# Attention keys stored in halves, and engine passes that take walked operands one half at a time

## The chip, the cores and the metric

The kernel runs on one core of one Trainium2 chip. The metric is the device time of one execution in microseconds (us). The core has TensorE (PE, with weight loads shown apart as PEld), VectorE (DVE), ScalarE (ACT), GpSimd (POOL) and SyncE (SP), which issues the transfers. PE writes into eight banks of PSUM; everything else lies in SBUF, 128 partitions deep.

## The reference

Two decoder layers over 256 tokens of width 1024, in float32. Layer 0 mixes tokens with a recurrent block, layer 1 with sparse attention; each is followed by a squared-ReLU MLP of width 4096, each sub-layer begins with an RMSNorm and ends with a residual add.

```python
# layer 0
proj = h @ w_in
y = gelu(proj[..., :D_RNN])
xb = conv4(proj[..., D_RNN:])                  # causal, depthwise
r = sigmoid(blockdiag(xb, w_a) + b_a); i = sigmoid(blockdiag(xb, w_x) + b_x)
a = exp(-8 * r * softplus(-lam)); u = sqrt(1 - a*a) * (i * xb)
x = x + (scan(a, u) * y) @ w_out
# layer 1: 16 heads in 4 groups, three branches, each with its own keys and values
s = q @ k.T * scale - slope * distance         # compressed, selected, window keys
o = g0 * softmax(s_c) @ v_c + g1 * softmax(s_s) @ v_s + g2 * softmax(s_w) @ v_w
x = x + o @ w_out
# after each
x = x + (relu(h @ w_up) ** 2) @ w_down
```

With 256 tokens all four blocks of 64 keys are selected and the window of 512 holds everything, so the selected and the window branch each see all causal keys. The compressed branch has 15 keys (16 with one of padding).

## The kernel before

**Products in split precision.** Activations lie transposed: model columns on partitions, tokens along the free axis. Each float32 operand is split into a high part (type float32r) and the rest. `mm3` (L328 to L330) multiplies high by high, high by low and low by high into one bank; `mm2` (L333, L335) does the same in two matmuls, where high and low parts lie side by side. Weights come by DMA into `raw`, a copy makes `whi`, a subtraction makes `wlo` (L278 and L287 in the MLPs, L341 and L338 in the planned sections; `copy` and `diff` are helpers, so many different passes carry L341 and L338).

**Walked operands.** A tile of 256 tokens is read by PE as 0, 128, 1, 129, and so on: one value of the first half, one of the second. `walk` and `walks` are that view, and `pairs` is the plain view with the same shape.

```python
def pairs(x):
    return x.rearrange("p (a i) -> p a i", i=2)
def walk(x):
    return x.rearrange("p (i a) -> p a i", i=2)
```

The bank then holds the tokens in the order 0, 128, 1, 129, ... Whoever reads it has to put them back: L679 (convolution input `xp`), L740 (gelu branch `y`), L796 (MLP up, `t`), L911 (queries), L923 (keys), L960 (keys and values before compression) read `pairs(z())`, multiply with `walk(rs)` (one over the norm, per token) and write `walk(...)`: they alternate between the halves at every value. In the other direction, tiles whose product shall come out in the plain order are stored so that the walk restores it: `xbh` and `xbl` (L341, L338 in `product`), `uhl` (L802, L803 after the up product), `oh` and `ol` (L341, L338 in `pv`).

**Sections.** The recurrent layer and the attention layer are each one `Section`: every operation is added to a planner with its engines, an assumed length in us, what it reads and writes, and a wished time. `emit` draws random offsets from a seed, makes a list schedule, improves it by backward and forward passes, takes the plan with the earliest end, and issues each engine's operations in that plan's order. Within an engine the order is then fixed, and engines wait for each other through semaphores. The MLPs are issued in program order: 32 pieces of the up product, each followed by `up_post` (L796, L801, L802, and L803 one piece later), then 8 x 4 pieces of the down product.

**End of the recurrent layer.** The `y` products come last. For each pair of chunks: L740 twice on DVE, gelu on ACT (L746), a product with the scan's result on DVE (L747), `xbh` (ACT or DVE) and `xbl` (DVE). The output projection needs all four pairs.

**Attention.** Per head three score products run (L1129 with the high part of the keys, L1130 with the low part): queries 0 to 127 against the first 128 keys of both branches and the compressed keys; queries 128 to 255 against the selected and the compressed keys; and against the window keys. Keys lie in `kh` and `kl`, group after group, in blocks of 128 keys in a row with the 16 compressed keys between them (`kset`, `kpair`, `kcomp`), and PE reads them in a row. DVE subtracts distances and finds the maximum from the bank (L1140; L1147 for compressed keys), ACT takes the exponential (L1143), DVE and ACT rescale (L1168, L1167), PE transposes (L1183), and `pv` (L1202) multiplies with values, two chunks of the output in one bank. `oh` and `ol` are made from that bank; the output projection of the last chunks waits for them.

Of the kernel before, what the change touches and what calls it, by code (L numbers as in the profile page):

```python
# [19 lines left out]
P = 128  # L20
# [199 lines left out]
def trunk_kernel(ctx: ExitStack, tc: tile.TileContext, x_in, vec_in, const_in, w2_in, wts, out):  # L220
# [320 lines left out]
    with ExitStack() as ph:  # L541
# [196 lines left out]
        def branch(m, t):  # L738
            z, zk = sec.proj("in", m, nextbank(), t, PJ)
            add("dve", 0.34, lambda e: e.tensor_tensor(walk(y_t[m]), pairs(z()), walk(rs), op=OP.mult), r=[zk, "rs"], w=[("y", m)], t=t + 2.6)  # L740

        def product(m, t):
            yk, hk, lk = keys("y", m), keys("xbh", m), keys("xbl", m)
            y, h, l_, x = (pair(z, m) for z in (y_b, xbhw, xblw, t_b))
            yw = y.rearrange("p k (a i) -> p k a i", i=2)
            add("act", 0.53, lambda e: e.activation(y, y, AF.Gelu_apprx_tanh), r=["tab"], w=yk, t=t)  # L746
# [37 lines left out]
    def mlp(layer, epilogue, first, last=None):  # L784
        with ExitStack() as ph:
# [4 lines left out]
            uhl = [up.tile([P, 2 * S], F32R, name="uhl", tag="uhl", bufs=NF) for _ in range(NF)]  # L790
            uh, ul = [walk(x[:, :S]) for x in uhl], [walk(x[:, S:]) for x in uhl]
            zrot = rotation(3, 4, 5, 0, 1, 2)

            def up_post(m, z):
                t = tmp.tile([P, S], F32, name="t", tag="t")
                dve.scalar_tensor_tensor(walk(t), pairs(z), 0.0, walk(rs), op0=OP.max, op1=OP.mult)  # L796
                flush()
# [3 lines left out]
                act.activation(u, t, AF.Square)  # L801
                act.activation(uh[m], pairs(t), AF.Square)  # L802
                later(lambda: dve.tensor_tensor(ul[m], pairs(u), uh[m].bitcast(F32), op=OP.subtract))  # L803

# [44 lines left out]
    with ExitStack() as ph:  # L849
# [15 lines left out]
        at.tile([P, 16], F32, name="edge0")  # L865
        GK, PC = 2 * S + NCP, P + NCP
        kh, kl = (at.tile([P, 4 * GK + NCP], F32R, name=n) for n in ("kh", "kl"))
        kpair = lambda y, g, n: y[:, g * GK:g * GK + 2 * (S + NCP)].rearrange("p (b k) -> p b k", b=2)[:, :, :n]
        kcomp = lambda y: y[:, :4 * GK].rearrange("p (g k) -> p g k", g=4)[:, :, P:PC]

        def kset(y, g, br):
            o, n = g * GK + br * (S + NCP), P if br else PC
            return y[:, o:o + 2 * n].rearrange("p (b k) -> p b k", b=2)[:, :, :P]
        two_blocks = lambda y: y.rearrange("p (b k) -> p b k", b=2)
# [30 lines left out]
        def qchunk(c, b, t, step):  # L905
# [4 lines left out]
            ak, bk = ("sa", c % NQ), ("sb", c % NQ)  # L910
            add("dve", 0.4, lambda e: e.scalar_tensor_tensor(walk(x), pairs(z()), cst[:, C_QS + c:C_QS + c + 1], walk(rs),  # L911
                                                             op0=OP.mult, op1=OP.mult), r=[zk, "rs"], w=[xk], t=t)
# [6 lines left out]
        def kchunk(gp, br, b, t, step):  # L919
            z, zk = proj_t(("ks", "kw")[br], gp, b, t, step)  # L920
            t += 4 * step
            x, xk, l_, lk = turn()
            add("dve", 0.34, lambda e, x=x: e.tensor_tensor(walk(x), pairs(z()), walk(rs), op=OP.mult), r=[zk, "rs"], w=[xk], t=t)  # L923
            x, l_ = two_blocks(x), two_blocks(l_)
# [31 lines left out]
        def cproj(i, gp, b, t, step):  # L956
            z, zk = proj_t(("ck", "cv")[i], gp, b, t, step)
            t += 4 * step
            x, xk, _, _ = turn()
            add("dve", 0.34, lambda e, x=x: e.tensor_tensor(walk(x), pairs(z()), walk(rs), op=OP.mult), r=[zk, "rs"], w=[xk], t=t)  # L960
            for hf in range(2):
# [144 lines left out]
        def scores(s, t):  # L1106
# [7 lines left out]
            a, cj = s // 4, s % 4  # L1114
            cview = lambda y, n, k: y[:, :2 * n].rearrange("p (b k) -> p b k", b=2)[:, :, :k]
            parts = ((0, lambda x: cview(x, PC, PC), lambda y: kpair(y, g, PC), (0, 1), 0.26),
                     (1, lambda x: x[:, :S + NCP], lambda y: y[:, g * GK:g * GK + S + NCP], (0,), 0.25),
                     (1, lambda x: x[:, :S], lambda y: y[:, g * GK + S + NCP:(g + 1) * GK], (1,), 0.23))
            for i, (qc, view, keys_, sets, d) in enumerate(parts):
# [12 lines left out]
                for b in sets:  # L1132
# [3 lines left out]
                    dist = cst[:, C_D0 + qc * P:C_D0 + qc * P + nk]  # L1136
                    src = (lambda z, b=b: cview(z(), PC, P)[:, b]) if qc == 0 else (
                        (lambda z: z()[:, :S]) if b else lambda z: cview(z(), PC, P))
                    shape = two_blocks if (qc, b) == (1, 0) else lambda y: y
                    add("dve", (0.2, 0.34)[qc], lambda e, z=z, src=src, shape=shape, dist=dist, row=row, j=j: e.tensor_tensor_reduce(  # L1140
                        shape(row), src(z), shape(dist), -slope, -NEG, OP.add, OP.min, mx[:, j:j + 1]),
                        r=bk + ["cst"], w=[mk, pk], t=t + 0.3)
# [3 lines left out]
                if 0 in sets:  # L1146
                    add("dve", 0.22, lambda e, z=z, qc=qc: e.tensor_tensor_reduce(  # L1147
                        css[a % 2][:, cj, qc], z()[:, P:PC], cst[:, C_DC + qc * NCP:C_DC + (qc + 1) * NCP], -slope, -NEG, OP.add,
                        OP.min, cmx[a % 2][:, 2 * cj + qc:2 * cj + qc + 1]),
# [288 lines left out]
```

## Time and profile before

| what | value |
|---|---|
| median of 3 runs | 562.9 us (562.57 to 563.83) |
| the profiled execution's own time | 563.95 us |
| its span, first to last instruction | 561.8 us |
| PE busy | 550.5 us (98%) |
| DVE busy | 436.3 us (78%) |
| ACT busy | 358.0 us (64%) |
| moved by DMA | 103.61 MB, mean 184 GB/s |
| granted PE clock over the span | 0.996 |

A matmul's length in the profile (about 276 ns for 256 columns) is longer than the distance to the next one, since matmuls overlap; the rate is read from the starts of successive ones. Passes of DVE and ACT overlap a little too, so that the next begins before the last has ended. Groups name a line, an engine, an operation, the tile written and the tiles read, the shape, the count, and then the busy time and the mean length of one in ns.

### The profile page before, as it was taken

The numbers are of one execution on the slowest core, as the hardware profiler recorded it, in microseconds if no ns is written. First come the engines' busy times: TensorE is split into PE (matmuls) and PEld (weight loads), VectorE is DVE, ScalarE is ACT, GpSimd is POOL, SyncE is SP. The second block draws the span as 40 slices with busy tenths as digits, with TensorE's granted clock in tenths as the row PEclk, the third lists the DMA queues.
The fourth block names the chain that finished last, engine by engine and source line by source line (L and its number), as shares of the span: only waits on it lengthen the run. The fifth ranks groups of instructions, "written<-read, shape, count | busy, mean of one in ns | idle before, by whom it ended". The sixth has DMA issues, their size and how long they took to land.

```text
span 561.8 us, 11456 instructions
## 1 busy us (share of the span) xinstructions
PE 550.5 (98%) x4422; PEld 528.5 (94%) x4422; DVE 436.3 (78%) x888; ACT 358.0 (64%) x670; POOL 40.1 (7%) x55
## 2 busy tenths in 40 slices
PE   9999899999999999999999999999999999999995
PEld 9989899999999999999899998989999999999995
DVE  6899999887788476476849999989988887465532
ACT  7699587777666354354646999977776765353321
POOL 1010000000000131131000000000000000142220
PEclk9999999999999999999999999999999999999998
DMA  8927266576566646655675432263586667556402
GB/s 313 409 90 226 83 225 215 174 234 200 191 194 222 223 161 214 225 167 198 219 229 177 143 104 58 76 211 99 200 239 200 191 213 234 182 187 218 158 1 76
DMA packets 33222, 103.61 MB, mean 184 GB/s; under 512 B 3856, under 2 KB 8080, under 8 KB 33168
## 3 DMA queue, kind: packets, MB, share of 16 engines
q1 hardware_dynamic: 32624, 102.42, 55.5%
q8 instruction: 35, 0.57, 0.4%
q10 hardware_dynamic: 544, 0.46, 0.2%
q14 instruction: 19, 0.16, 0.1%
HBM read 99.23 MB, written 1.05 MB: 179 GB/s over the span
## 4 chain that ended last, share of the span: by engine, by line
PE 73%; DVE 18%; DMA 5%; ACT 2%; issue 1%; SPq 0%; POOL 0%; DVEq 0%; ACTq 0%; POOLq 0%
PE bank L333 19%; PE bank L329 13%; PE bank L330 13%; PE bank L328 13%; PE bank L335 9%; DVE wlo L338 4%; DMA raw<-in_dram 3%; DVE pt L1140 2%; DMA gw<-in_dram 2%; DVE pt L1168 2%; DVE xb L683 1%; DMA pt<-tt 1%; DVE tt L911 1%; DVE t L735 1%; PE bank L1036 1%
## 5 line engine op out<-in xcount | busy, mean ns | idle before, releaser
L328 PE MATMUL bank<-hhl,whi 128*128 128x256 f32 x768 | 212.0, 276 | 0.4 <-DVE tt L960 0.4
L330 PE MATMUL bank<-hhl,wlo 128*128 128x256 f32 x768 | 211.5, 275 | 0.0
L329 PE MATMUL bank<-hhl,whi 128*128 128x256 f32 x768 | 211.5, 275 | 0.0
L333 PE MATMUL bank<-uhl,whi 128*128 128x512 f32 x480 | 157.3, 382 | 0.0
L328 PEld LDWEIGHTS bank<-hhl,whi 128*128 128x128 f32 x768 | 147.7, 192 | 0.6 <-DVE tt L960 0.4
L330 PEld LDWEIGHTS bank<-hhl,wlo 128*128 128x128 f32 x768 | 147.7, 192 | 0.0
L329 PEld LDWEIGHTS bank<-hhl,whi 128*128 128x128 f32 x768 | 147.7, 192 | 0.0
L287 DVE TENSOR_TENSOR wlo<-raw,whi 128x1024 fp32r<-128x1024 f32 x115 | 142.8, 1262 | 1.9 <-ACT whi L278 1.9
L335 PE MATMUL bank<-uhl,wlo 128*128 128x256 f32 x480 | 130.8, 273 | 0.0
L278 ACT CAST whi<-raw 128x1024 fp32r<-128x1024 f32 x116 | 120.0, 1056 | 14.1 <-ACT whi L278 11.0
L333 PEld LDWEIGHTS bank<-uhl,whi 128*128 128x128 f32 x480 | 90.7, 189 | 12.6
L335 PEld LDWEIGHTS bank<-uhl,wlo 128*128 128x128 f32 x480 | 92.2, 192 | 0.0
L338 DVE TENSOR_TENSOR wlo<-raw,whi 128x1024 fp32r<-128x1024 f32 (+2 forms) x72 | 77.1, 1091 | 1.9 <-ACT whi L341 1.8
L341 ACT CAST whi<-raw 128x1024 fp32r<-128x1024 f32 (+2 forms) x64 | 61.1, 969 | 15.4 <-DMA raw<-in_dram 7.3
L538 DVE TENSOR_TENSOR xt<-xt,bank 128x256 f32<-128x256 f32 x54 | 22.3, 419 | 62.2 <-PE bank L335 60.2
L796 DVE SCALAR_TENSOR_TENSOR t<-bank,rstd 128x256 f32<-128x256 f32 x64 | 39.5, 622 | 22.7 <-PE bank L330 22.6
L801 ACT ACTIVATE u<-t 128x256 f32<-128x256 f32 x64 | 26.7, 417 | 45.1 <-DVE t L796 44.9
L803 DVE TENSOR_TENSOR uhl<-u,uhl 128x256 fp32r<-128x256 f32 x64 | 40.8, 638 | 2.7 <-ACT uhl L802 2.6
L802 ACT ACTIVATE uhl<-t 128x256 fp32r<-128x256 f32 x64 | 42.5, 664 | 0.0
L514 ACT ACTIVATE hhl<-xt,vec 128x256 fp32r<-128x256 f32 x8 | 4.1, 508 | 41.4 <-DVE xt L538 41.4
L1143 ACT ACTIVATE pt<-pt,mx 128x128 f32<-128x128 f32 (+1 forms) x64 | 28.6, 449 | 2.0 <-DVE mx L1140 2.0
L1295 ACT ACTIVATE xg<-xt,vec 128x256 f32<-128x256 f32 x7 | 3.6, 508 | 37.7 <-DVE xt L538 37.7
(206 smaller groups left out, 764.1 us busy)
## 6 DMA issues: line engine op xcount, KB each, us to landing
raw<-in_dram SPq DMA_DIRECT2D x171, 512.0 KB, 4.3
raw<-in_dram SPq DMA_DIRECT2D x4, 560.0 KB, 4.5
gw<-in_dram SPq DMA_DIRECT2D x4, 512.0 KB, 9.2
raw<-in_dram SPq DMA_DIRECT2D x6, 256.0 KB, 4.9
y<-in_dram SPq DMA_DIRECT2D x2, 512.0 KB, 7.5
pT<-in_dram SPq DMA_DIRECT2D x2, 512.0 KB, 6.9
xt<-in_dram SPq DMA_DIRECT2D x3, 256.0 KB, 4.9
kl<-tl SPq DMA_DIRECT2D x8, 64.0 KB, 3.8
```

Of the source, the lines that this page charges most:

```text
L278: (act.copy if eng is None else eng.tensor_copy)(hi_t[i % NSPL][:, :n], raw_of(i)[:, :n])
L287: (eng or dve).tensor_tensor(lo[:, :n], raw_of(i)[:, :n], hi[:, :n].bitcast(F32), op=OP.subtract)
L328: pe.matmul(ps, wh, xh, start=start, stop=False)
L329: pe.matmul(ps, wh, xl, start=False, stop=False)
L330: pe.matmul(ps, wl, xh, start=False, stop=stop)
L333: pe.matmul(ps.rearrange("p (h a i) -> p h a i", h=2, i=2), wh, xhl.rearrange("p (h i a) -> p h a i", h=2, i=2), start=start, stop=False)
L335: pe.matmul(pairs(ps[:, S:]), wl, xh, start=False, stop=stop)
L338: return lambda e: e.tensor_tensor(o, a, h.bitcast(F32), op=OP.subtract)
L341: return lambda e: (e.copy if e is act else e.tensor_copy)(o, a)
L796: dve.scalar_tensor_tensor(walk(t), pairs(z), 0.0, walk(rs), op0=OP.max, op1=OP.mult)
L802: act.activation(uh[m], pairs(t), AF.Square)
L803: later(lambda: dve.tensor_tensor(ul[m], pairs(u), uh[m].bitcast(F32), op=OP.subtract))
```

## The change

It has two parts. First, every DVE or ACT pass with a walked operand keeps its data where they were and changes the order in which it goes through them. `evens` reads or writes all even places and then all odd ones; `parts` takes the first half and then the second. A pass that alternated between the halves of its SBUF tile and read a bank in a row now goes through the tile in a row and through the bank (or the other tile) at every second value. Second, the keys are stored in halves of a region of 272 places per group and branch: all even keys, and 136 places further all odd keys, the compressed keys in front of the selected ones in the same manner. The score products read the two halves alternately, which gives the plain order in the bank; the DVE passes on scores then read one run, where the first of queries 128 to 255 read two blocks. In the planner the assumed lengths of two of the three score products fall by 0.01.

```diff
+    def evens(x):
+        return x.rearrange("p (a i) -> p i a", i=2)
+    def parts(x):
+        return x.rearrange("p (i a) -> p i a", i=2)
...
-            add("dve", 0.34, lambda e: e.tensor_tensor(walk(x[:, 3:]), pairs(z()), walk(rs), op=OP.mult), r=[zk, "rs"], w=[xk], t=t)
+            add("dve", 0.34, lambda e: e.tensor_tensor(parts(x[:, 3:]), evens(z()), parts(rs), op=OP.mult), r=[zk, "rs"], w=[xk], t=t)
...
-            add("dve", 0.34, lambda e: e.tensor_tensor(walk(y_t[m]), pairs(z()), walk(rs), op=OP.mult), r=[zk, "rs"], w=[("y", m)], t=t + 2.6)
+            add("dve", 0.34, lambda e: e.tensor_tensor(parts(y_t[m]), evens(z()), parts(rs), op=OP.mult), r=[zk, "rs"], w=[("y", m)], t=t + 2.6)
...
-            y, h, l_, x = (pair(z, m) for z in (y_b, xbhw, xblw, t_b))
-            yw = y.rearrange("p k (a i) -> p k a i", i=2)
+            y, h, l_, x = (pair(z, m) for z in (y_b, xbh_b, xbl_b, t_b))
+            yw = y.rearrange("p k (a i) -> p k i a", i=2)
+            h, l_ = (z.rearrange("p k (i a) -> p k i a", i=2) for z in (h, l_))
...
-                dve.scalar_tensor_tensor(walk(t), pairs(z), 0.0, walk(rs), op0=OP.max, op1=OP.mult)
+                dve.scalar_tensor_tensor(parts(t), evens(z), 0.0, parts(rs), op0=OP.max, op1=OP.mult)
...
-                act.activation(uh[m], pairs(t), AF.Square)
-                later(lambda: dve.tensor_tensor(ul[m], pairs(u), uh[m].bitcast(F32), op=OP.subtract))
+                act.activation(uhp[m], evens(t), AF.Square)
+                later(lambda: dve.tensor_tensor(ulp[m], evens(u), uhp[m].bitcast(F32), op=OP.subtract))
...
+        KR, HC = S + NCP, NCP // 2
+        kh, kl = (at.tile([P, 8 * KR], F32R, name=n) for n in ("kh", "kl"))
+        kpair = lambda y, g: y[:, 2 * g * KR:2 * (g + 1) * KR].rearrange("p (r i q) -> p r q i", r=2, i=2)[:, :, :PC // 2]
+        kcomp = lambda y: y.rearrange("p (g r i q) -> p g r q i", g=4, r=2, i=2)[:, :, 0, :HC]
+        def kregion(y, g, br):
+            o = (2 * g + br) * KR
+            return y[:, o:o + KR].rearrange("p (i q) -> p i q", i=2)
+        def kplain(y, g, br):
+            o = 0 if br else HC
+            return kregion(y, g, br)[:, :, o:o + P]
+        def kall(y, g, br):
+            return kregion(y, g, br)[:, :, :P if br else P + HC].rearrange("p i q -> p q i")
...
-                add(HI, copy(kset(kh, g, br), x), r=[xk], w=[("k", g, br), ("k", g, br, 1)], t=t + 0.5)
+                add(HI, copy(kplain(kh, g, br), evens(x)), r=[xk], w=[("k", g, br), ("k", g, br, 1)], t=t + 0.5)
...
-            parts = ((0, lambda x: cview(x, PC, PC), lambda y: kpair(y, g, PC), (0, 1), 0.26),
-                     (1, lambda x: x[:, :S + NCP], lambda y: y[:, g * GK:g * GK + S + NCP], (0,), 0.25),
-                     (1, lambda x: x[:, :S], lambda y: y[:, g * GK + S + NCP:(g + 1) * GK], (1,), 0.23))
+            parts = ((0, lambda x: x[:, :2 * PC].rearrange("p (r q i) -> p r q i", r=2, i=2), lambda y: kpair(y, g), (0, 1), 0.25),
+                     (1, lambda x: pairs(x[:, :KR]), lambda y: kall(y, g, 0), (0,), 0.24),
+                     (1, lambda x: pairs(x[:, :S]), lambda y: kall(y, g, 1), (1,), 0.23))
...
-            ow = lambda: o().rearrange("p (k a i) -> p k a i", k=n, i=2)
+            ow = lambda: o().rearrange("p (k a i) -> p k i a", k=n, i=2)
...
-            add([("act", 0.1 + 0.24 * n, 0.0), ("dve", 0.07 + 0.27 * n, 0.2)], lambda e: copy(ohw[:, oj], ow())(e), r=bk, w=ok,
+            add([("act", 0.1 + 0.24 * n, 0.0), ("dve", 0.07 + 0.27 * n, 0.2)], lambda e: copy(ohp[:, oj], ow())(e), r=bk, w=ok,
...
-            add("dve", 0.07 + 0.27 * n, lambda e: diff(olw[:, oj], ow(), ohw[:, oj])(e), r=bk + ok, w=lk, t=t + 1.9 * n + 0.3)
+            add("dve", 0.07 + 0.27 * n, lambda e: diff(olp[:, oj], ow(), ohp[:, oj])(e), r=bk + ok, w=lk, t=t + 1.9 * n + 0.3)
```

The passes L911, L923 and L960 change in the same way as the one of `y`.

More of the change, by code (lines that the diff above doesn't have):

```diff
@@ L791, in mlp @@
             uh, ul = [walk(x[:, :S]) for x in uhl], [walk(x[:, S:]) for x in uhl]
+            uhp, ulp = [parts(x[:, :S]) for x in uhl], [parts(x[:, S:]) for x in uhl]
             zrot = rotation(3, 4, 5, 0, 1, 2)
@@ L865, in trunk_kernel @@
         at.tile([P, 16], F32, name="edge0")
[L866 to L874, printed above, removed]
+        PC = P + NCP
+        KR, HC = S + NCP, NCP // 2
[10 more added lines that the diff above has]
+            return kregion(y, g, br)[:, :, :P if br else P + HC].rearrange("p i q -> p q i")
         at.tile([P, 16], F32, name="edge1")
@@ L878, in trunk_kernel @@
         ohw, olw = (walks(x.rearrange("p (k s) -> p k s", s=S)) for x in (oht, olt))
+        ohp, olp = (x.rearrange("p (k i a) -> p k i a", i=2, a=P) for x in (oht, olt))
         oh, ol = ([x[:, i] for i in range(8)] for x in (ohw, olw))
@@ L910, in qchunk @@
             ak, bk = ("sa", c % NQ), ("sb", c % NQ)
-            add("dve", 0.4, lambda e: e.scalar_tensor_tensor(walk(x), pairs(z()), cst[:, C_QS + c:C_QS + c + 1], walk(rs),
+            add("dve", 0.4, lambda e: e.scalar_tensor_tensor(parts(x), evens(z()), cst[:, C_QS + c:C_QS + c + 1], parts(rs),
                                                              op0=OP.mult, op1=OP.mult), r=[zk, "rs"], w=[xk], t=t)
@@ L922, in kchunk @@
             x, xk, l_, lk = turn()
-            add("dve", 0.34, lambda e, x=x: e.tensor_tensor(walk(x), pairs(z()), walk(rs), op=OP.mult), r=[zk, "rs"], w=[xk], t=t)
-            x, l_ = two_blocks(x), two_blocks(l_)
+            add("dve", 0.34, lambda e, x=x: e.tensor_tensor(parts(x), evens(z()), parts(rs), op=OP.mult), r=[zk, "rs"], w=[xk], t=t)
             for hf in range(2):
                 g = gp * 2 + hf
-                add(HI, copy(kset(kh, g, br), x), r=[xk], w=[("k", g, br), ("k", g, br, 1)], t=t + 0.5)
-            add("dve", 0.34, diff(l_, x, kset(kh, gp * 2, br)), r=[xk, ("k", gp * 2, br), ("k", gp * 2, br, 1)], w=[lk], t=t + 1)
+                add(HI, copy(kplain(kh, g, br), evens(x)), r=[xk], w=[("k", g, br), ("k", g, br, 1)], t=t + 0.5)
+            add("dve", 0.34, diff(parts(l_), evens(x), kplain(kh, gp * 2, br)), r=[xk, ("k", gp * 2, br), ("k", gp * 2, br, 1)], w=[lk], t=t + 1)
             for hf in range(2):
                 own, oth, g = own_(hf), own_(1 - hf), gp * 2 + hf
-                move(kset(kh, g, br)[oth], kset(kh, g, br)[own], [("k", g, br)], [("k", g, br, 1)], t + 0.8)
-                move(kset(kl, g, br)[own], l_[own], [lk, "kl"], [("k", g, br, 2)], t + 1.2)
+                move(kplain(kh, g, br)[oth], kplain(kh, g, br)[own], [("k", g, br)], [("k", g, br, 1)], t + 0.8)
+                move(kplain(kl, g, br)[own], l_.rearrange("p (i q) -> p i q", i=2)[own], [lk, "kl"], [("k", g, br, 2)], t + 1.2)
         def kkeys(g, br):
@@ L959, in cproj @@
             x, xk, _, _ = turn()
-            add("dve", 0.34, lambda e, x=x: e.tensor_tensor(walk(x), pairs(z()), walk(rs), op=OP.mult), r=[zk, "rs"], w=[xk], t=t)
+            add("dve", 0.34, lambda e, x=x: e.tensor_tensor(parts(x), evens(z()), parts(rs), op=OP.mult), r=[zk, "rs"], w=[xk], t=t)
             for hf in range(2):
@@ L997, in kc_out @@
                 r=["hid"] + ck, w=[("ps", 6)], t=t)
-            o4 = lambda: o().rearrange("p (g n) -> p g n", g=4)
+            o4 = lambda: o().rearrange("p (g q i) -> p g q i", g=4, i=2)
             add("act", 0.1, lambda e: e.copy(kcomp(kh), o4()), r=[("ps", 6)], w=["kch"], t=t)
@@ L1114, in scores @@
             a, cj = s // 4, s % 4
-            cview = lambda y, n, k: y[:, :2 * n].rearrange("p (b k) -> p b k", b=2)[:, :, :k]
-            parts = ((0, lambda x: cview(x, PC, PC), lambda y: kpair(y, g, PC), (0, 1), 0.26),
-                     (1, lambda x: x[:, :S + NCP], lambda y: y[:, g * GK:g * GK + S + NCP], (0,), 0.25),
-                     (1, lambda x: x[:, :S], lambda y: y[:, g * GK + S + NCP:(g + 1) * GK], (1,), 0.23))
+            parts = ((0, lambda x: x[:, :2 * PC].rearrange("p (r q i) -> p r q i", r=2, i=2), lambda y: kpair(y, g), (0, 1), 0.25),
+                     (1, lambda x: pairs(x[:, :KR]), lambda y: kall(y, g, 0), (0,), 0.24),
+                     (1, lambda x: pairs(x[:, :S]), lambda y: kall(y, g, 1), (1,), 0.23))
             for i, (qc, view, keys_, sets, d) in enumerate(parts):
@@ L1136, in scores @@
                     dist = cst[:, C_D0 + qc * P:C_D0 + qc * P + nk]
[L1137 to L1141, printed above, removed]
+                    so = (0 if qc else PC) if b else NCP
+                    add("dve", (0.2, 0.34)[qc], lambda e, z=z, so=so, nk=nk, dist=dist, row=row, j=j: e.tensor_tensor_reduce(
+                        row, z()[:, so:so + nk], dist, -slope, -NEG, OP.add, OP.min, mx[:, j:j + 1]),
                         r=bk + ["cst"], w=[mk, pk], t=t + 0.3)
@@ L1147, in scores @@
                     add("dve", 0.22, lambda e, z=z, qc=qc: e.tensor_tensor_reduce(
-                        css[a % 2][:, cj, qc], z()[:, P:PC], cst[:, C_DC + qc * NCP:C_DC + (qc + 1) * NCP], -slope, -NEG, OP.add,
+                        css[a % 2][:, cj, qc], z()[:, :NCP], cst[:, C_DC + qc * NCP:C_DC + (qc + 1) * NCP], -slope, -NEG, OP.add,
                         OP.min, cmx[a % 2][:, 2 * cj + qc:2 * cj + qc + 1]),
```

## The prediction, made before the result was known

> **What bounds the kernel now.** I read the page's busy line first, then the waits of TensorE (PE), then the busy time by stretches.
>
> ```profile
> span 561.8 us, 11456 instructions
> ...
> PE 550.5 (98%) x4422; PEld 528.5 (94%) x4422; DVE 436.3 (78%) x888; ACT 358.0 (64%) x670; POOL 40.1 (7%) x55
> ```
>
> PE works through the whole span; only time that PE does not need or does not lose can leave the total. What it loses to other engines is listed by the view of waits (engine and line, what it waited for, total, times, longest):
>
> ```profile
> PE bank L329 <- DVE xbl L338: 1.2, 2, 1.0
> PE bank L329 <- DVE ol L338: 0.7, 1, 0.7
> PE bank L328 <- ACT xbh L341: 0.5, 1, 0.5
> PE bank L1036 <- DVE tt L960: 0.4, 1, 0.4
> PE bank L328 <- DVE tt L960: 0.4, 1, 0.4
> ...
> PE bank L1129 <- DVE cm L1147: 0.3, 1, 0.3
> ```
>
> All six waits are for operations that this change rewrites, or for a VectorE (DVE) queue that holds such operations. The stretches (us; busy time of PE, PEld, DVE, ACT, POOL with counts) say where that can matter:
>
> ```profile
> 65.60:72.50 6.90, 5.18 (x41) 4.46 (x39) 6.90 (x10) 3.99 (x5) 0.00 (x0) 1.00 0.71 230
> ...
> 95.00:180.00 85.00, 85.00 (x751) 84.64 (x750) 71.96 (x101) 60.36 (x99) 0.00 (x0) 1.00 0.62 203
> ...
> 372.50:377.00 4.50, 3.68 (x32) 3.05 (x29) 3.41 (x4) 3.50 (x4) 0.00 (x0) 1.00 0.96 353
> ```
>
> In the first (end of the recurrent layer) DVE is busy throughout and PE is not; in the second (up half of the first MLP) PE is busy throughout; in the third (end of attention) PE idles while ACT and DVE take turns.
>
> **The change part by part: the engines' order.** The groups by shape give the price of a walked pass (mean ns of one after the busy time):
>
> ```profile
> L803 DVE TENSOR_TENSOR uhl<-u,uhl 128x256 fp32r<-128x256 f32 x64 | 40.8, 638 | 2.7 <-ACT uhl L802 2.6
> L796 DVE SCALAR_TENSOR_TENSOR t<-bank,rstd 128x256 f32<-128x256 f32 x64 | 39.5, 622 | 22.7 <-PE bank L330 22.6
> L538 DVE TENSOR_TENSOR xt<-xt,bank 128x256 f32<-128x256 f32 x54 | 22.3, 419 | 62.2 <-PE bank L335 60.2 <-PE bank L330 1.4
> L740 DVE TENSOR_TENSOR y<-bank,rstd 128x256 f32<-128x256 f32 x8 | 4.9, 618 | 0.0
> L338 DVE TENSOR_TENSOR xbl<-y,xbh 128x512 fp32r<-128x512 f32 x4 | 4.4, 1099 | 0.1
> L338 DVE TENSOR_TENSOR ol<-bank,oh 128x512 fp32r<-128x512 f32 x4 | 4.4, 1093 | 1.1 <-ACT oh L341 1.1
> ```
>
> ```profile
> L802 ACT ACTIVATE uhl<-t 128x256 fp32r<-128x256 f32 x64 | 42.5, 664 | 0.0
> L801 ACT ACTIVATE u<-t 128x256 f32<-128x256 f32 x64 | 26.7, 417 | 45.1 <-DVE t L796 44.9
> L341 ACT CAST oh<-bank 128x512 fp32r<-128x512 f32 x4 | 4.4, 1093 | 0.2 <-PE bank L1202 0.2
> L341 ACT CAST xbh<-y 128x512 fp32r<-128x512 f32 x3 | 3.4, 1132 | 3.6 <-DVE y L747 3.6
> L746 ACT ACTIVATE y<-y 128x512 f32<-128x512 f32 x4 | 2.5, 632 | 3.1 <-DVE y L740 3.0
> ```
>
> L538 reads a bank too and has as many values as L740, but no operand is walked: 419 against 618 ns. On ACT, L801 and L802 square the same tile; the walked output costs 664 against 417. So jumping between the two halves at every value costs about 0.20 us per 256 values on DVE and 0.25 on ACT. After the change the same values go to the same places, one half at a time: outputs are written and rstd is read in a row, and the other operand (bank, t, u, y) is read at every second value. No row of this trace reads at every second value, so I bound it: from below by the unwalked rows (419 DVE, 417 ACT, a gain of 0.20 to 0.25), from above by a second penalty of the walk's size (about 0.82 on DVE, a loss of 0.20). I take the unwalked price: a step of two values is far nearer to neighbours than to a jump of 128, and the walked row is what happens at 128.
>
> [...]
>
> Where does it land? In the up halves, 64 groups save 0.4 us of DVE and 0.25 of ACT each, some 26 and 16 us of busy time, and I count **nothing**: PE is busy for 85.00 of 85.00 us there and no wait of PE in the list names L796, L802 or L803. What is covered stays covered, by PE's own 2.7 us per piece.
>
> **End of the recurrent layer.** These rows of the timeline (start, length) are PE's stall and the queue that makes it:
>
> ```profile
> 65.56 0.28 PE L330 MATMUL bank<-xbh,wlo 128*128 128x256 f32 x1
> 66.31 0.38 PE L328 MATMUL bank<-xbh,whi 128*128 128x256 f32 x1 [0.48 <-ACT xbh L341]
> 67.72 0.38 PE L329 MATMUL bank<-xbl,whi 128*128 128x256 f32 x1 [1.03 <-DVE xbl L338]
> ```
>
> ```profile
> 52.70 0.69 DVE L722 SCALAR_TENSOR_TENSOR t<-a,t 128x512 f32<-128x512 f32 x1
> ...
> 61.90 0.62 DVE L740 TENSOR_TENSOR y<-bank,rstd 128x256 f32<-128x256 f32 x1
> 62.35 1.11 DVE L338 TENSOR_TENSOR xbl<-y,xbh 128x512 fp32r<-128x512 f32 x1
> 63.30 1.22 DVE L338 TENSOR_TENSOR wlo<-raw,whi 128x1024 fp32r<-128x1024 f32 x1
> 64.43 0.68 DVE L747 TENSOR_TENSOR y<-y,t 128x512 f32<-128x512 f32 x1
> 65.03 0.61 DVE L740 TENSOR_TENSOR y<-bank,rstd 128x256 f32<-128x256 f32 x1
> ...
> 66.61 1.06 DVE L338 TENSOR_TENSOR xbl<-y,xbh 128x512 fp32r<-128x512 f32 x1
> ```
>
> ```profile
> 52.05 0.61 ACT L721 ACTIVATE a<-r 128x512 f32<-128x512 f32 x1
> ...
> 65.14 1.11 ACT L341 CAST xbh<-y 128x512 fp32r<-128x512 f32 x1 [1.95 <-DVE y L747]
> ```
>
> Start to start a walked 256 takes 0.45 (61.90 to 62.35) and a walked 512 takes 0.95; an unwalked 512 takes 0.60 (64.43 to 65.03), so 0.07 of its 0.674 length overlaps, and an unwalked 256 is worth 0.35 at most. I use a saving of 0.12 per 256 and 0.35 per 512. What DVE saves before 52.70 I count at nothing, because L722 starts as ACT's L721 ends (52.66), and ACT's work up to there is not changed. After it, two y passes (the one at 61.90 and one just before) and the xbl at 62.35 save 0.59, so L747 ends at 64.52 instead of 65.11; ACT's xbh, 0.63 long by L746's row, is done at 65.2, before PE asks at 65.67. One more y pass makes 0.71: the second xbl runs from 65.90 to 66.57, and PE goes on at 66.62 instead of 67.72. That is **1.1**. The other of the two xbl waits (1.2 less 1.0, and the restart) is met by further savings: **0.3**. Sum 1.4. The MLP behind it has no wait to eat this up.
>
> **Into attention.** Two waits of 0.4 are for L960, a y-like pass. The first shrinks by the pass's own 0.2, the second (behind a key copy and two more such passes) by about 0.3: **0.5**. The 0.3 for L1147 stands behind an ol pass on DVE: **0.2**.
>
> **The score products.** Their operands are read in a row now, the projections' are walked:
>
> ```profile
> 330.37 0.29 PE L1130 MATMUL bank<-kl,sb 128*128 128x288 f32 x1
> ...
> 331.00 0.27 PE L328 MATMUL bank<-hhl,whi 128*128 128x256 f32 x1
> ...
> 332.34 0.82 PE L1183 MATMUL bank<-cst,pt 128*128 128x128 f32 x6
> ```
>
> From 330.37 to 331.00 five products with 288, 256, 256, 272 and 272 columns pass: 1344 columns in 0.63 us, 0.469 ns each. From 331.00 to 332.34 twelve walked products pass: 3072 columns in 1.34 us, 0.436 ns. The 16 heads have 2 x (288 + 272 + 256) columns each, 26112 in all: at 0.033 ns less, **0.85**. Rounding of the starts is worth 0.2, so I take 0.7; from below the bound is 0 (the halves of keys stand 136 values apart, not 128, and the price of that distance is not in these rows). The score readers on DVE keep their sizes and read in a row as before. The key copies now read every second value; the DVE ones may cost 0.13 more each if they drop to the price of a subtraction, on the few that DVE takes; the DMAs of keys keep their number and bytes.
>
> **End of attention.**
>
> ```profile
> 373.48 1.06 ACT L341 CAST oh<-bank 128x512 fp32r<-128x512 f32 x1
> 374.57 1.09 DVE L338 TENSOR_TENSOR ol<-bank,oh 128x512 fp32r<-128x512 f32 x1 [1.09 <-ACT oh L341]
> 375.71 0.38 PE L329 MATMUL bank<-ol,whi 128*128 128x256 f32 x1 [0.74 <-DVE ol L338]
> ```
>
> Here nothing covers: oh, then ol, then PE. With L746's 0.63 oh ends at 374.11; ol, at the unwalked 0.67, at 374.81; PE goes on at 374.86: **0.85**.
>
> **Sum.** 1.4 + 0.5 + 0.2 + 0.7 + 0.85 = 3.65. The profiled execution took 563.95 us (561.8 of span and 2.15 around it): 560.3. It stood 1.05 above the median 562.9, so against the median the forecast is **559.2**.
>
> **The rivals.** First, *the attention part's order is drawn anew*: the planned lengths of two of three score products fall by 0.01, and the planner orders a whole section from such numbers, so its queues may change throughout. For it: DVE and ACT both fill this part, so a new order has little slack. Against: most lengths and all dependencies stay. Price: the bank wait of 0.3 before L1129, at twelve of sixteen heads instead of one, is 3.3 us; 562.5, and past sixteen heads and other waits 564.5.
>
> Second, *reading the bank at every second value keeps the walk's price*. For it: no row shows such a read. Against: the place where the walk costs on ACT's L802 is an SBUF tile. Then y, L960, oh and ol stay, xbl and xbh gain: xbl runs from 66.26 to 66.93, PE resumes at 66.98 (0.74), the second wait gives 0.2, the scores 0.7. Sum 1.65: 561.2. [...]
>
> Third, **slower**: *that read costs a second penalty*, 0.82 us per 256 values of a bank. Eight xp passes grow by 1.6 us before ACT's chain begins, and some 1.2 of it reaches PE's stall at 67.72; oh and ol at the tail add 0.8; L960 0.6; twelve q and key passes and three ol add 3.6 us to a full DVE, of which PE would see about 1.5; less 0.7 for scores and 0.6 for xbl: plus 2.8, 565.7. It decides from about 0.70 us per pass, a third of the way from the walked to the bound. Against it: a full bank read in a row runs at SBUF's speed (419).
>
> Fourth, *the keys in halves do not run faster* at a distance of 136: 559.9.
>
> **How the numbers follow.** Forecast 0.55, new order 0.15, bank price kept 0.16, bank price doubled 0.10, keys no faster 0.04. About 0.2% (1.1 us) is what a measurement of this kernel tells from no change. Faster than 561.8: 0.53 of the forecast, 0.12, 0.03, 0 and 0.04 make 0.72; within: 0.02, 0.04, 0.06, 0.01, 0.13; slower: 0.06 of the new order and 0.09 of the doubled price, 0.15. The forecast's own range is 557.2 (all waits named above gone) to 560.8; the range over the cases is 557.2 to 563.6, which leaves out the doubled price, the worst orders and a little below.
>
> **What would show it.** L796 and L740 at 420 to 440 ns, L802 near 417, xbl near 675: the engines' step; 600 or more for those that read a bank: the second or third rival. Score products at 0.11 a piece of 256 columns. No wait of PE for xbh and under 0.4 for xbl and ol together. PE waits at L1129 at many heads: the first rival. Up halves that get shorter than 85 us of PE in any way would prove wrong that they are worth nothing.

## The result and the profile after

| | before | after |
|---|---|---|
| median of 4 runs | 563.16 us (562.57 to 563.83) | 557.6 us (557.33 to 557.95) |
| ratio | | 0.9901, 95% interval 0.9884 to 0.9918 |
| span of the profiled execution | 561.8 us | 556.1 us |
| PE, DVE, ACT busy | 550.5, 436.3, 358.0 us | 547.5, 414.7, 350.0 us |

The kernel became 5.6 us faster, within the forecast's own range (557.2 to 560.8) and 1.6 us below the predicted 559.2. Against the 21 runs of before that were taken beside the experiment order_only (median 562.6) it is 5.0 us. The waits of PE after the change (all but the one for the warm-up tile at the start) no longer hold xbh, xbl, oh or ol:

```profile
PE bank L1143 <- DVE cm L1159: 0.4, 1, 0.4
PE bank L1192 <- DVE sq L1106: 0.3, 1, 0.3
PE bank L1005 <- DVE rstd L452: 0.3, 1, 0.3
PE bank L334 <- DVE tt L975: 0.3, 1, 0.3
PE bank L1318 <- ACT sqh L1315: 0.2, 1, 0.2
```

The groups by shape of the changed kernel (mean ns of one behind the busy time; new line numbers: L804 was L796, L811 was L803, L746 was L740, L810 and L809 were L802 and L801, L344 and L347 were L338 and L341):

```profile
L811 DVE TENSOR_TENSOR uhl<-u,uhl 128x256 fp32r<-128x256 f32 x64 | 27.9, 436 | 3.3 <-ACT uhl L810 3.3
L804 DVE SCALAR_TENSOR_TENSOR t<-bank,rstd 128x256 f32<-128x256 f32 x64 | 26.9, 423 | 37.1 <-PE bank L336 36.8
L746 DVE TENSOR_TENSOR y<-bank,rstd 128x256 f32<-128x256 f32 x8 | 3.3, 416 | 0.0
L344 DVE TENSOR_TENSOR xbl<-y,xbh 128x512 fp32r<-128x512 f32 x4 | 2.9, 736 | 0.0
L344 DVE TENSOR_TENSOR ol<-bank,oh 128x512 fp32r<-128x512 f32 x4 | 2.7, 685 | 0.1
```

```profile
L810 ACT ACTIVATE uhl<-t 128x256 fp32r<-128x256 f32 x64 | 31.3, 489 | 0.0
L809 ACT ACTIVATE u<-t 128x256 f32<-128x256 f32 x64 | 26.6, 416 | 50.9 <-DVE t L804 50.8
L347 ACT CAST oh<-bank 128x512 fp32r<-128x512 f32 x4 | 2.3, 581 | 2.0 <-PE bank L1214 2.0
L347 ACT CAST xbh<-y 128x512 fp32r<-128x512 f32 x3 | 2.4, 796 | 3.5 <-DVE y L754 3.5
```

All passes above that read a bank at every second value cost about what an unwalked pass of before costs (423 and 416 ns against 419, 685 against 674 on DVE; 581 against 632 on ACT). Those that read an SBUF tile at every second value are a little dearer: 436 against 419 and 736 (xbl) against the 674 of before's L747 on DVE, and on ACT 489 against 416 and 796 (xbh) against the 632 of before's L746.

The end of the recurrent layer, PE and then DVE: of the stall between 65.56 and 67.72, a quarter of a microsecond is left.

```profile
65.33 0.28 PE L334 MATMUL bank<-xbh,whi 128*128 128x256 f32 x1
65.70 0.38 PE L335 MATMUL bank<-xbl,whi 128*128 128x256 f32 x1
```

```profile
51.74 0.69 DVE L728 SCALAR_TENSOR_TENSOR t<-a,t 128x512 f32<-128x512 f32 x1 [0.27 <-ACT a L727]
...
64.91 0.73 DVE L344 TENSOR_TENSOR xbl<-y,xbh 128x512 fp32r<-128x512 f32 x1
```

And a head's score products: from 300.79 to 301.49 six products with 1632 columns pass in 0.70 us, 0.429 ns a column, against 0.469 before; they are as fast as the walked products of the projections (0.436 in before).

```profile
300.79 0.29 PE L1143 MATMUL bank<-kh,sa 128*128 128x288 f32 x1
...
301.49 0.28 PE L334 MATMUL bank<-hhl,whi 128*128 128x256 f32 x1
```

For the experiments I cut each profile at PE's own landmarks and took the difference of starts (us): the out projection of the recurrent layer from the first product with xbh to the last with xbl (before: 65.00 to 89.81), the attention entry from the transposed norms (L990 before) to the first product with kh (270.61 to 304.23), the score section from there to the last product with kl (362.63), and the tail from there to the last product with ol (382.85). The first MLP, from the last xbl to the transposed norms, takes 180.80 in every kernel here. The sections come from one profiled execution of each kernel, the medians from several.

| kernel | median | ratio to before, 95% | first xbh at | out projection | entry | score section | tail |
|---|---|---|---|---|---|---|---|
| before | 562.6 to 563.2 | 1 | 65.00 | 24.8 | 33.6 | 58.4 | 20.2 |
| after | 557.60 | 0.9901 (0.9884 to 0.9918) | 64.66 | 22.4 | 32.9 | 56.4 | 19.9 |
| order_only | 557.92 | 0.9911 (0.9897 to 0.9924) | 64.60 | 22.6 | 32.8 | 57.1 | 19.0 |
| keys_only | 563.25 | 1.0002 (0.9993 to 1.0011) | 64.52 | 24.8 | 34.0 | 57.9 | 20.8 |
| old_lengths | 557.64 | 0.9906 (0.9893 to 0.9920) | 64.33 | 22.8 | 32.8 | 56.7 | 19.1 |
| mlp_only | 562.88 | 1.0001 (0.9992 to 1.0010) | 64.84 | 24.8 | 32.9 | 58.4 | 20.1 |
| rg_only | 560.53 | 0.9961 (0.9949 to 0.9973) | 64.51 | 22.8 | 33.0 | 58.4 | 20.2 |
| rg_no_xp | 560.83 | 0.9966 (0.9954 to 0.9978) | 64.58 | 23.0 | 33.0 | 58.4 | 20.1 |
| att_only | 560.46 | 0.9954 (0.9942 to 0.9966) | 64.13 | 24.8 | 32.9 | 57.1 | 19.2 |
| ohol_only | 561.17 | 0.9973 (0.9963 to 0.9983) | 64.75 | 24.8 | 33.7 | 57.7 | 19.1 |
| pe_extra | 560.68 | 0.9966 (0.9953 to 0.9978) | 64.03 | 22.7 | 33.1 | 59.1 | 19.9 |
| seed_185 | 557.80 | 0.9913 (0.9899 to 0.9926) | 63.86 | 22.9 | 32.9 | 56.4 | 19.9 |
| seed_187 | 560.10 | 0.9955 (0.9941 to 0.9969) | 64.38 | 22.7 | 34.2 | 57.0 | 20.2 |

The last three columns hold the same products only where the attention part has the order of before. In after, keys_only, pe_extra and the two seeds twelve products of the output projection, 1.34 us at 0.112 us from start to start, stand in the tail instead of the score section (193 products from the last kl to the last ol, 181 in the others). In seed_187 twelve projection products more stand in the entry. Between kernels of different order only the sum of these sections can be compared.

### The profile page after: what moved, and what is told of

Read it like the earlier page. It is cut to its first block, busy times and chain, and to the rows that moved or that the text cites. A ratio compares the mean times of both kernels' runs of the same rounds, so it can differ in the third digit from the quotient of the medians.

```text
span 556.1 us, 11510 instructions
## 1 busy us (share of the span) xinstructions
PE 547.5 (98%) x4422; PEld 527.6 (95%) x4422; DVE 414.7 (75%) x886; ACT 350.0 (63%) x672; POOL 39.6 (7%) x55
## 3 DMA queue, kind: packets, MB, share of 16 engines
HBM read 99.23 MB, written 1.05 MB: 180 GB/s over the span
## 4 chain that ended last, share of the span: by engine, by line
PE 87%; DVE 7%; ACT 4%; issue 1%; POOL 0%; DVEq 0%; ACTq 0%; POOLq 0%
PE bank L339 19%; PE bank L334 16%; PE bank L335 16%; PE bank L336 16%; PE bank L341 9%; PE bank L1214 2%; PE bank L1195 1%; DVE wlo L344 1%; PE bank L589 1%; DVE t L741 1%; PE bank L1051 1%; PE bank L1143 1%; PE bank L1144 1%; ACT t L718 1%; PE bank L1053 1%; PE bank L1052 1%
## 5 line engine op out<-in xcount | busy, mean ns | idle before, releaser
L341 PE MATMUL bank<-uhl,wlo 128*128 128x256 f32 x480 | 130.8, 273 | 0.0
L278 ACT CAST whi<-raw 128x1024 fp32r<-128x1024 f32 x116 | 118.3, 1040 | 14.5 <-ACT whi L278 11.0
L341 PEld LDWEIGHTS bank<-uhl,wlo 128*128 128x128 f32 x480 | 92.2, 192 | 0.0
L344 DVE TENSOR_TENSOR wlo<-raw,whi 128x1024 fp32r<-128x1024 f32 (+2 forms) x72 | 77.1, 1089 | 2.6 <-ACT whi L347 2.3
L347 ACT CAST whi<-raw 128x1024 fp32r<-128x1024 f32 (+2 forms) x64 | 61.1, 969 | 14.4 <-PE bank L335 6.0
L544 DVE TENSOR_TENSOR xt<-xt,bank 128x256 f32<-128x256 f32 x54 | 22.4, 418 | 62.9 <-PE bank L341 60.7
L809 ACT ACTIVATE u<-t 128x256 f32<-128x256 f32 x64 | 26.6, 416 | 50.9 <-DVE t L804 50.8
L804 DVE SCALAR_TENSOR_TENSOR t<-bank,rstd 128x256 f32<-128x256 f32 x64 | 26.9, 423 | 37.1 <-PE bank L336 36.8
L810 ACT ACTIVATE uhl<-t 128x256 fp32r<-128x256 f32 x64 | 31.3, 489 | 0.0
L811 DVE TENSOR_TENSOR uhl<-u,uhl 128x256 fp32r<-128x256 f32 x64 | 27.9, 436 | 3.3 <-ACT uhl L810 3.3
L1155 ACT ACTIVATE pt<-pt,mx 128x256 f32<-128x256 f32 (+1 forms) x64 | 28.6, 451 | 1.5 <-DVE mx L1152 1.0
```

Source lines behind the costliest of these rows:

```text
L278: (act.copy if eng is None else eng.tensor_copy)(hi_t[i % NSPL][:, :n], raw_of(i)[:, :n])
L341: pe.matmul(pairs(ps[:, S:]), wl, xh, start=False, stop=stop)
L344: return lambda e: e.tensor_tensor(o, a, h.bitcast(F32), op=OP.subtract)
L347: return lambda e: (e.copy if e is act else e.tensor_copy)(o, a)
L810: act.activation(uhp[m], evens(t), AF.Square)
L811: later(lambda: dve.tensor_tensor(ulp[m], evens(u), uhp[m].bitcast(F32), op=OP.subtract))
```

## The experiments

### The two parts apart, and the planned lengths

order_only takes all engine passes of the change and leaves keys and planned lengths; keys_only does the opposite; old_lengths is the whole change with the planned lengths of before.

```diff
 order_only: before, with
-... walk(y_t[m]), pairs(z()), walk(rs) ...
+... parts(y_t[m]), evens(z()), parts(rs) ...
 (and so for xp, xbh, xbl, t, uhl, tt, oh, ol)
 keys_only: after, with each of these put back to walk and pairs
 old_lengths: after, with
-    lambda y: kpair(y, g), (0, 1), 0.25)      lambda y: kall(y, g, 0), (0,), 0.24)
+    lambda y: kpair(y, g), (0, 1), 0.26)      lambda y: kall(y, g, 0), (0,), 0.25)
```

> All engine passes in the new order, keys and planned lengths as before, so the queues keep the order of before. My theory (the gain is PE's waits for the rewritten passes): the recurrent layer's end gives 2.4 to 2.7 us as in the changed kernel (not the 1.4 I had forecast), the attention entry 0.8, the tail about 0.9, the middle 0.5; about 4.7 us less than before, 558.4. Rival (the keys or the new draw of the order carry a large part): 2.7 us less or so, 560.5, with the score section as long as before.

> Keys in halves and the two shorter planned lengths, walked passes as before. My theory: 0.7 us from the score products and a draw of the order that is worth nothing on average: 0.3 to 1.2 us less than before, 562.4, recurrent layer unchanged. Rival (the new draw of the order is what shortened the score section by 2 us): 2 us less, 561.

> The changed kernel with the planned lengths of the score products as before (0.26 and 0.25). If the shorter lengths only redraw the order without a gain: within 0.6 us of the changed kernel, 557.6. If the draw carried the unexplained 1.4 us of the score section: 558.5 to 559.5.

Measured: order_only takes 4.7 us off (557.92), keys_only nothing that can be told (563.25, ratio 1.0002; I had expected 0.3 to 1.2), old_lengths is the changed kernel over again (557.64). The engines' order carries the result. The halves of the keys make the score section 0.4 us shorter (57.1 to 56.7, order_only against old_lengths, with the same products in it) and the median 0.3, with intervals that overlap. The shorter planned lengths do redraw the order: of the 886 passes that DVE issues about 126 stand elsewhere in the sequence, all in attention. In the profiles the score section and the tail together take 76.3 us with that draw and 75.8 without (old_lengths); in the medians the draw is worth 0.0. In keys_only, where the passes are still walked, the list of waits is longer than before's, and score section and tail together take 78.7 us against 78.6. Waits that took back what the faster products gave are the likely reason; that is argued from one profile.

```profile
PE bank L335 <- DVE xbl L344: 1.2, 2, 1.1
PE bank L335 <- DVE ol L344: 0.9, 2, 0.7
PE bank L1050 <- DVE tt L974: 0.8, 1, 0.8
...
PE bank L1213 <- ACT pc L347: 0.5, 1, 0.5
PE bank L1142 <- DVE cm L1158: 0.4, 1, 0.4
```

### The passes by place

```diff
 mlp_only:  before, with t, uhl (three passes after each up product) in the new order
 rg_only:   before, with xp, y, xbh, xbl in the new order
 rg_no_xp:  rg_only, with xp put back
 att_only:  before, with tt (queries, keys, compressed projections), oh, ol in the new order
 ohol_only: before, with oh and ol alone
```

> Only the three passes after each up product in the new order. My theory: DVE falls by about 24 us and ACT by about 11 us of busy time and the time does not change, 0.0 to 0.2 us less than before. Rival (faster passes in the up halves free weights or banks earlier): 0.6 us less or more.

> Only the recurrent layer's passes (xp, y, xbh, xbl) in the new order. Theory (PE's stall at its end goes whole): last xbl product 2.4 to 2.7 us earlier and the time 2.4 us less than before, 560.3. Rival (what is won there is given back in attention, whose entry hangs on transfers and not on PE): 1.5 us less or under.

> As the one before, but the convolution's input xp stays walked. If what DVE saves before the ACT pass at 52 us is worth nothing, as I had counted: the same 2.4 us less, 560.3. If xp's saving goes through ACT's earlier start: 0.6 to 1.0 us of it is missing, 561.1, with the multiply after ACT's square starting near 52.7 us as before instead of 51.7.

> Only attention's passes (q, k, compressed projections, oh, ol) in the new order, keys as before. Theory: the three parts add up, so what is left of the 4.7 us of all passes: 2.0 to 2.6 us less than before, 560.4, of which about 1.2 in the tail between the last score product and the last ol product. Rival (the score section is paced by PE and these passes only give back what the recurrent layer's earlier end made possible): under 1.5 us less.

> Of attention's passes only oh and ol in the new order, all else as before. They are all of the tail's 1.0 us and, through the ol passes in the middle, part of the score section's 1.3: 1.4 us less than before, 561.4. If the score section's gain is theirs too: 2.3 us less, 560.5.

Measured: mlp_only 562.88 (1.0001), rg_only 560.53 (2.3 us less), att_only 560.46 (2.4 less); 2.3 and 2.4 make order_only's 4.7. The up halves were bought for nothing, as counted: 15.6 us of DVE and 6.2 of ACT less than before, and no time. I had expected 24 and 11 from the lengths of the passes. But passes overlap: from the start of a `t` or `uhl` pass on DVE to the next start (medians) it was 0.46 and 0.48 us in before and is 0.34 and 0.35 in mlp_only. So a walked pass of 256 held its queue 0.12 us longer, not 0.20, and 128 of them make the 15.6.

```profile
PE 549.7 (98%) x4422; PEld 527.5 (94%) x4422; DVE 420.7 (75%) x888; ACT 351.8 (63%) x670; POOL 39.8 (7%) x55
```

rg_no_xp stands at 560.83, 0.3 us above rg_only, with overlapping intervals; in the profiles the out projection is 0.2 longer. So xp's saving before ACT's square at 52 us is worth 0.2 to 0.3 us, which the medians cannot tell from nothing, and not the 0.6 to 1.0 that I expected of the rival. That L728 starts 0.96 earlier in the changed kernel (51.74 against 52.70) is mostly not its doing: rg_no_xp has it at 52.27 with xp walked, and rg_only only 0.27 earlier, at 52.00.

```profile
52.27 0.69 DVE L728 SCALAR_TENSOR_TENSOR t<-a,t 128x512 f32<-128x512 f32 x1 [0.16 <-ACT a L727]
```

ohol_only is 1.5 us faster in the medians; in its profile the tail is 1.1 shorter and the score section 0.75. The rest of att_only's score section (0.6) belongs to the query and key passes; the two accounts do not differ enough for more.

mlp_only and rg_only show something about the attention entry. Their L960 pass (L967 there) is as walked as before, yet their entries are 32.9 and 33.0, as short as the changed kernel's, and before's wait at L1036 is not in rg_only's list:

```profile
PE bank L335 <- DVE ol L344: 0.7, 1, 0.7
PE bank L335 <- DVE xbl L344: 0.5, 1, 0.5
PE bank L334 <- DVE tt L967: 0.4, 1, 0.4
...
```

In the profile of before that pass waited for a transfer out of the tile that it overwrites; in mlp_only the pass of the same place, 1.6 us earlier, waited for nothing, and in ohol_only it waited for the transfer again:

```profile
277.03 0.60 DVE L960 TENSOR_TENSOR tt<-bank,rstd 128x256 f32<-128x256 f32 x1 [1.40 <-DMA pt<-tt]
```

```profile
275.39 0.60 DVE L967 TENSOR_TENSOR tt<-bank,rstd 128x256 f32<-128x256 f32 x1
```

```profile
276.88 0.60 DVE L967 TENSOR_TENSOR tt<-bank,rstd 128x256 f32<-128x256 f32 x1 [1.48 <-DMA pt<-tt]
```

So the wait comes and goes with the landing of a transfer. Of the six profiled kernels in which this pass is walked, three have it (before 1.40, keys_only 1.74, ohol_only 1.48 on DVE; PE then loses 0.4 to 0.8 at the line of L1036, and the entry takes 33.6 to 34.0), and three do not (32.9 to 33.0). Of the seven with the pass rewritten, two wait for the transfer on DVE (att_only 1.06, seed_187 0.28) and none loses time on PE at that line. Where the transfer lands in time, the walked pass thus costs no more than the rewritten one. Whether the rewriting makes a late landing harmless is not shown.

The profiled execution of before stood 1.05 us above the median. This wait is some 0.7 of it. Its start is late too: its first product with xbh is at 65.00, the other twelve kernels' between 63.86 and 64.84, five of them with xp walked as before.

### What PE's time in the score section is worth

```diff
 pe_extra: after, with
+                    if 0 in sets:
+                        e.matmul(view(z()), x[:, qs], keys_(kl), start=True, stop=True)
                     e.matmul(view(z()), x[:, qs], keys_(kh), start=True, stop=False)
```

> The changed kernel, with two of the three score products of each head done once more beforehand (its result is overwritten): 32 products of 288 and 272 columns, 3.8 us of PE. If PE's time in the score section reaches the end whole: 3.8 us more than the changed kernel, 561.4. If, as the keys' part suggests (0.87 us saved by the products' own starts, 0.3 us in the time), only a third does: 1.3 us more, 558.9; the rest shows as less waiting of PE in the score section.

Measured: 560.68, 3.1 us above the changed kernel for 3.8 us of added products; the score section grew by 2.6 us and the waits at L1143 and L1192 are gone from the list. PE's added time there reaches the end by about four fifths. My "a third" was wrong, and if saved time counts like added time, the halves of the keys should be worth about 0.7 us rather than the 0.3 seen. The medians cannot tell these apart; that the key copies became dearer on ACT (402 to 452 ns) goes in the right direction and is small. It stays open.

### Another draw of the order

```diff
-SEEDS, ROUNDS, SHIFT = (64, 186), 6, 1.5
+SEEDS, ROUNDS, SHIFT = (64, 185), 6, 1.5      and 187
```

> The changed kernel with another seed for the attention section's plan: how much a new draw of the order is worth. If the draw is nearly free, as the planned lengths' change was: within 0.6 us of 557.6. My first rival had 2 to 5 us more.

> A second other seed: within 0.6 us of 557.6 if the draw is nearly free; 2 to 5 us more by my first rival.

Measured: 557.80 and 560.10. One draw costs nothing, the other 2.5 us. Its list has two long waits of PE, the first of which stands at 0.3 in the changed kernel and the second in no other:

```profile
PE bank L1192 <- DVE sq L1106: 1.0, 1, 1.0
PE bank L1195 <- DVE pt L1180: 0.8, 1, 0.8
```

So a new order can cost what the first rival has at its lower end, if at other lines than the L1129 that it named, and the change's own draw did not meet it.

### The price of a walked pass, by side

The ladder adds passes of 128 values to the changed kernel where DVE and ACT have room.

```diff
 ladder: after, in the last MLP's down half, five times
+        dve.tensor_tensor(po, step(db, 1), b[:, :P], op=OP.mult)           # bank, step 1
+        dve.tensor_tensor(po, step(db, 2), b[:, :P], op=OP.mult)           # step 2, then 4
+        dve.tensor_tensor(plain(po), halves(db), plain(b), op=OP.mult)     # alternating read
 (the same from an SBUF tile; the same with act.activation(..., AF.Square))
+        dve.tensor_tensor(halves(po), plain(flat), plain(b), op=OP.mult)   # alternating output
```

> The changed kernel with 18 additional passes of 128 values at five places of the last MLP's down half, where DVE and ACT have room; their results go nowhere. DVE multiplies a bank or an SBUF tile with a tile in a row, ACT squares, each at steps of 1, 2 and 4 values, alternating between halves, and with an alternating output. [...] If the changed kernel's rows tell the rule: bank step 2 as cheap as step 1 on both engines, SBUF step 2 dearer by 0.1 ns a value on DVE and 0.3 on ACT, alternating dearer by 0.8 and 1.0. Where the price falls, on the read or on the write, is open.

Measured in one execution, first DVE (L1343: bank, step 1; L1345: step 4; L1346: alternating; L1347 to L1350: SBUF, step 1, 2, 4, alternating; L1351: alternating output), then ACT (L1352: bank, step 1; L1354: step 4; L1356 to L1359: SBUF, step 1, 2, 4, alternating; L1360: alternating output):

```profile
L1349 DVE TENSOR_TENSOR probed<-hhl 128x128 f32<-128x128 f32 x5 | 2.4, 471 | 0.2
L1351 DVE TENSOR_TENSOR probed<-hhl 128x128 f32<-128x128 f32 x5 | 2.0, 397 | 0.2
L1348 DVE TENSOR_TENSOR probed<-hhl 128x128 f32<-128x128 f32 x5 | 1.6, 311 | 0.2
L1350 DVE TENSOR_TENSOR probed<-hhl 128x128 f32<-128x128 f32 x5 | 1.5, 293 | 0.2
L1347 DVE TENSOR_TENSOR probed<-hhl 128x128 f32<-128x128 f32 x5 | 1.5, 292 | 0.2
...
L1345 DVE TENSOR_TENSOR probed<-bank,hhl 128x128 f32<-128x128 f32 x5 | 1.5, 291 | 0.2
L1346 DVE TENSOR_TENSOR probed<-bank,hhl 128x128 f32<-128x128 f32 x5 | 1.5, 291 | 0.2
L1343 DVE TENSOR_TENSOR probed<-bank,hhl 128x128 f32<-128x128 f32 x5 | 1.4, 282 | 0.0
```

```profile
L1358 ACT ACTIVATE probea<-hhl 128x128 f32<-128x128 f32 x5 | 2.8, 560 | 0.2
L1360 ACT ACTIVATE probea<-hhl 128x128 f32<-128x128 f32 x5 | 2.2, 439 | 0.2
L1357 ACT ACTIVATE probea<-hhl 128x128 f32<-128x128 f32 x5 | 1.8, 359 | 0.2
L1359 ACT ACTIVATE probea<-hhl 128x128 f32<-128x128 f32 x5 | 1.7, 340 | 0.2
L1356 ACT ACTIVATE probea<-hhl 128x128 f32<-128x128 f32 x5 | 1.5, 309 | 0.2
...
L1354 ACT ACTIVATE probea<-bank 128x128 f32<-128x128 f32 x5 | 1.4, 278 | 0.2
L1352 ACT ACTIVATE probea<-bank 128x128 f32<-128x128 f32 x5 | 1.3, 267 | 0.0
```

An alternating output lengthens a pass of 128 values by 105 ns on DVE and 130 on ACT, 0.8 and 1.0 ns a value, which is all of the walked passes' price of before (203 and 247 per 256). Reading SBUF alternately costs nothing on DVE (293 against 292) and 31 ns on ACT. A bank costs nearly the same at every step and in every order: 291 against 282 in a row on DVE, 278 to 279 against 267 on ACT, where the passes in a row are the first of each series. Reading SBUF at step 2 costs 19 and 50 ns, at step 4 179 and 251. The halves lie 64 values apart here and 128 in the kernel; that the price is the same per value (0.8 ns on DVE, 1.0 on ACT) speaks for the same cause.

## Why the prediction was right, and where it was off

**The engines' order: right, with the price on the wrong side.** I took the price for one of jumping, on either side of a pass. The ladder puts it on the output: per 128 values alternating outputs cost 105 ns on DVE and 130 on ACT, alternating SBUF reads nothing on DVE and 31 ns on ACT. The sum did not suffer, because the change takes the jump from the output. xbl came to 736 ns and not to 675, which fits the ladder's 19 ns per 128 values for reading SBUF at every second one (76 per 512, on 674). The second and third rivals (a bank read at every second value keeps or doubles the price) fall with 416 to 423 ns for L746 and L804 and with the ladder's bank rows: at step 2, at step 4 and in alternation a bank is dearer than in a row by 9 to 12 ns per 128 values (291 against 282 on DVE, 278 to 279 against 267 on ACT).

**Up halves at nothing: right.** mlp_only, 1.0001.

**End of the recurrent layer, forecast 1.4: rg_only 2.3 in the medians, 2.0 in its out projection.** The first term (1.1) holds: in rg_no_xp PE resumes at 66.19 instead of 67.72 with everything before it 0.42 earlier, 1.1 net. The term that was too small is "the other of the two xbl waits: 0.3". The rest of the out projection gave 0.7: 24.8 less 23.0 is 1.8, less 1.1. I had read 0.2 off the list of waits. The rows of before show what that list leaves out:

```profile
71.17 0.28 PE L329 MATMUL bank<-xbl,whi 128*128 128x256 f32 x1
71.41 0.38 PE L330 MATMUL bank<-xbh,wlo 128*128 128x256 f32 x1
...
71.95 0.28 PE L328 MATMUL bank<-xbh,whi 128*128 128x256 f32 x1
72.44 0.38 PE L329 MATMUL bank<-xbl,whi 128*128 128x256 f32 x1 [0.21 <-DVE xbl L338]
```

Where nothing holds it, the next of these products of 256 columns starts 0.11 us after the last (in before at 71.62, 71.73, 71.84 and 71.95); the list counts idle time only from that one's modelled end, 0.28 after its start. The second gap lost 0.49 less 0.11, 0.38 us, of which 0.21 is listed; the first lost 0.13 and is not listed at all. PE waited there for a `wlo` that DVE ended at 71.35 (started at 70.14, 1.21 long), behind a walked y pass. The next start behind each of the two gaps came 0.10 late as well, and a third xbl at 77.99 cost 0.2. In rg_no_xp about 0.15 of these 0.9 is left, so that the starts account for the 0.7. "Nothing before 52.70" was nearly right: xp is worth 0.2 to 0.3, which the medians do not tell from nothing.

**Into attention, forecast 0.5 for L960: open, and nothing where a transfer lands in time.** The wait at L1036 came with the late landing of a transfer. It is in the profiles of before, keys_only and ohol_only; mlp_only, rg_only and rg_no_xp lose it with the pass still walked. The other wait, at L328, went from 0.4 to 0.3. The prediction took the length of the pass for the cause of both.

**The middle, forecast 0.2: 1.3** (att_only, 58.4 to 57.1). The same mistake as in the recurrent layer: the list held one wait of 0.3 there. The starts show the rest. Both kernels issue the same 543 products in the same order in this section, and at eight places the next start comes later in before than in att_only: by 0.52 at 330.16, where the list has its 0.3, and by 0.08 to 0.16 at seven places that are not in the list, 1.3 in all. One of the seven, in before and then in att_only, with 0.28 and 0.12 from start to start:

```profile
362.15 0.28 PE L1130 MATMUL bank<-kl,sb 128*128 128x256 f32 x1
362.43 0.36 PE L1129 MATMUL bank<-kh,sb 128*128 128x272 f32 x1
```

```profile
359.41 0.28 PE L1137 MATMUL bank<-kl,sb 128*128 128x256 f32 x1
359.53 0.29 PE L1136 MATMUL bank<-kh,sb 128*128 128x272 f32 x1
```

Which pass released each of the seven is not shown.

**The tail, forecast 0.85: 1.0** (att_only; ohol_only 1.1). Right in mechanism and nearly in size: PE's gap before ol shrinks by 0.6 in att_only, short gaps ahead of it give the rest, and oh and ol measured 581 and 685 ns against the 630 and 670 assumed. In the changed kernel itself the tail is 0.3 shorter, with twelve more products in it and no wait for ol in the list.

**The score products, forecast 0.7: 0.3 in the medians, not told from nothing nor from 0.7.** Their own rate fell as forecast, 0.469 to 0.429 ns a column.

**The new order, first rival at 0.15:** it did not cost anything here in the medians, and 2.5 us for one of two other seeds. (In the lists of chances "faster" and "within", the second figure belongs to the kept bank price and the third to the new order; the totals are right.)

Summed by medians: 2.3 in the recurrent layer, 2.4 in attention and 0.3 for the keys make 5.0. That is the whole change against the before taken with the experiments (562.6 less 557.6), and 5.0 of the 5.6 against the one taken with the result. The forecast had 1.4, 1.55 and 0.7 for the same three. It was short by gaps that the list of waits leaves out (0.4 and 1.1) and too high for the keys and perhaps for L960, so that some errors cancelled. That the time lies in the range is partly luck: the lower end 557.2 is called "all waits named above gone", but the six waits listed make 3.5 us and the scores 0.85, which gives 558.55, above the measured 557.6.

## What to carry to other kernels

In this kernel a permutation between engines was best placed where a bank is read: every order tried there was free within 12 ns per 128 values on DVE and ACT, while an output that alternates between two places made a pass longer by 0.8 to 1.0 ns a value, of which the DVE queue saw about 0.5 (0.12 us per 256 in mlp_only). Faster passes were worth what PE had lost to them (15.6 us of DVE in the up halves took nothing off the time), and PE's losses are read from the starts of successive products, not from the list of waits, which omits what lies under a product's modelled end (in the score section it held 0.3 of 1.3 us). Sections between two landmarks can be compared only where they hold the same products. A wait behind a transfer in one profiled execution should be looked for in other profiles before it is counted as a gain; this one stood in three of six.

## What was not expected of the hardware

PE read faster in alternation: a head's score products that alternate between halves 136 values apart ran at 0.429 ns a column in after, those that read in a row in before at 0.469. DVE and ACT paid for alternating outputs (397 against 292 ns and 439 against 309 per 128 values). Alternating SBUF reads were free on DVE although successive values lie 64 places apart (293 against 292), and yet reads at step 4 of the same tile cost 1.4 ns a value more on DVE (471 against 292 per 128) and 2.0 on ACT (560 against 309). The bank at steps 2 and 4 and in alternation cost 9 to 12 ns per 128 values more than in a row (291 against 282, 278 to 279 against 267).
